# A gated residual tail in another order: two gate products recorded ahead of an out-projection, and a last pair of its own

## The chip, the cores and the metric

The kernel runs on one core of a Trainium2 chip. The metric is the device time of one execution in microseconds (us); a comparison uses the median of several runs. The engines are TensorE (PE; its weight loads are shown apart as PEld), VectorE (DVE), ScalarE (ACT), GpSimd (POOL), and SyncE (SP), whose queue starts every transfer of this kernel.

## The reference, cut to what matters

One decoder layer over 1024 tokens of width 1024, in float32. The last part of it is what the change touches:

```
proj = rms_norm(x) @ w_in                       # split into the columns of both head groups
o_a  = gated delta rule (4 heads, chunks of 64) * silu(a_z)
o_b  = sparse attention (top 256 keys, 8 heads) * silu(b_z)
x = x + concat([o_a, o_b], -1) @ w_out
gate = sigmoid(rms_norm(x) @ w_ple_gate + b_ple_gate)
x = x + (p @ w_ple) * gate
```

## The kernel before, in words

Everything is kept transposed: 128 channels on the partitions, tokens along the free axis, in two halves of 512 tokens (n = 0 and n = 1). A float32 matrix product is made from three products in a fast format: each operand is split into a high part and a low part (`hi`, `lo`; ACT copies the high part, POOL or DVE subtracts to get the low one), and `mm3` issues hi x hi, hi x lo, lo x hi. A product over 512 channels is four `mm3`, so 12 matmuls of 512 columns.

**Out-projection.** `out_job` makes one block of 128 output channels in two parts: the part over the delta-rule heads (jobs oA0 to oA7 for the first half, oC0 to oC7 for the second) and the part over the attention heads (oB0 to oB7, and oD0 to oD7). Jobs oA, oC and oB are fill: they run on PE among the attention's own products. The jobs oD need the attention's last block of 128 queries. That last block ends in `fin`: ACT and DVE bring the sums out of PSUM into `ot`, POOL multiplies by `zt`, ACT makes the high part (`mch` in the trace), POOL the low part (`mcl`).

**Gate.** The gate projection (1024 by 1024) is made for four pairs of output blocks, j = 0 to 3. In each pair, two output blocks and two halves of the tokens form a 2 by 2 block product, done with seven products of 12 matmuls in place of eight (c1 to c7). Two of them, c7 (weights `s3`, tokens `t3`) and c3 (weights `s4`, tokens `b22`), need the first half of the tokens alone: `gate_pre`. The weights `s1` to `s4` are sums and differences of four raw weight blocks r11, r12, r21, r22, made on POOL (`mixed`, tile `mixl`), then split (`sh`, `sl`); `a11`, `a12`, `a22` are raw blocks split as they are (`hiw`, `low`). `f1` and `f2` are intermediate sums that stay in the ring of three `mixl` buffers until `s1` and `s2` are split. `gate_out` finishes a 128 by 512 block: add a part, scale by the row norm, tanh on ACT, two DVE steps, store.

**Order.** Nothing is issued while the Python program runs. It records operations (`Plan.add`), with edges for every data and buffer hazard, and then issues them in a written-out order: `TURNS` is a packed list of 7561 numbers, each the index of the next operation among those still left. Each engine's queue follows that one order. A buffer ring is filled in recorded order, not in issued order. Opening and closing of a buffer pool are operations of that list too:

```
for o in deps:                       # Plan.mark: a pool's closing depends on each use of its tiles
    self.edge(o, op, 2)
...
for k, m in self.marks.items():      # and every opening or closing comes behind the last ones
    self.edge(m, op, 2 if k == key else 0)
...
assert all(p in seen for p in o.pre) # Plan.run: no operation is issued ahead of what it depends on
```

So an operation on a tile of the pool `tail` (`self.tp`: the tiles rawg, sh, sl, p1, u, v) is issued, on its engine, behind every operation of that engine on tiles of the attention's pools, `ot` among them. `raww`, `hiw`, `low` and `mixl` lie in older pools and are not bound by this.

Of the kernel before, what the change touches and what calls it, by code (L numbers as in the profile page):

```python
# [8 lines left out]
F32 = mybir.dt.float32  # L9
# [11 lines left out]
T = 1024  # L21
# [91 lines left out]
Xv*_Jx=wE?kRxU{3>M}1y=xL$+#TGfg_$2g?+FPyxev31O!yRk`hT7l;A#F;Y;g>w(v*cT#^q(VWoM(=<?8k<E-NFO(|s+|nem=0OGf0(|CXuGk+ZF_Oh%V&Nz2rs>4|Wj
$&Tij3M00BI+0AGc_n3UerPRYy~(O7G+2?Q?HWP{i~h>gzocY|snI!9QIUlXAf|!#j3ht657hT5d+5JCq%HDvS8T(!7L^t@Ph0QT7T}hxmKof!E#a8KeOvH?9qYGyxB1Fi
i(6WJt$0gIYogs7YV&RiZ45Q{R!@a0x%KOVp|w-}ZBwCvb)ji;%a&R$-&DPfW14cwqWOJAG)HE6#ymshN%xa&Pgbp5*)(x%as4sRqSPW!M$aSe6Z3{oxS!}fe*Cy9d1A=5
3|;D3z1*{mSUT1|>KoZsJJve7X_Odk85zl$8e2$g9ZigmT=HCm_%q%W8@%U5Pt94;zp?hTJ9a9%R2MJRk()+yLVb8yQ0tCqo!h+yt%M!wngg@2c(*RzjhY6|VrPujdCV!O
KV_)iiZ(;}_y+QEQhS_iuWEy>0B_#ZoZHk4u%(T)jeG24D;y+P#uE1vQ?s**I~&4t27>)N`thuRfdR6#ug_8*0d%1yh$Y6B7&9@qvA^Gpt%)M&daOTGJE+UVYBmySY_O96
crhS5JspI*Z3ep!xLU9_h$3b@f*7zF15)VkhLuQinV|Dcy5YDB-+&SY1e&l-;<->|Q6X(8yTOf6>)=|4ZYXSr6OfZET#$1kF12UP(uh7h6jp~q_LV_7u-vZkSv4N}fIdB4
6N_1qs7Be+NiZa4v}S1H@${T_F<Z22?OK~u7nMrPVab%`(X>IS#VIyno^T!}^AWOEo5H+mgUTFnI-F*`*RI0+o}kXA59C26o~dyg(%q;GW6qdKt+z)+8)eO~)-V=K=Z?4m
1Dy)~nNjvy%#R{^vlRUACgF$rB$P`+v?c(2Wol7fVkXJ=S@pN8NR>`U7MQ-0ZzSKz%QGat%)H6Sca-h6EOM`FxtF<HVFfR~5SDK8eEPNYbpDEzbMaD6&IOtlF3`NBdP+Pc  # L120
M#Qjq9C4g;P)y^a8D2I<L3TgMkU8Z!fCA<U633G`PU9&^NbXA5Dy~L_+D4QIz13RniusM&2JI4(YDUTaMxwWYsGrZ(Q{A;x6BVuQi>jI<6|AJHOR6Z=SLCap7=|jPrMOg>
Bh4W`mt+z;ok&J$o<(TN>B1cjgryl9!yq&bWC{R+kO)DmB?yjCIDzAo64fRWiSlx)thu?Fx(kL8HM(3`6b()>(`a-Avw=u6K^3XZ$th{F=d`qr>{&3fuXo=&@BW|yWdYIw
KwBH#+nYgBv6wcS%*xW_4Y%eYorX9;I9mvsZlsk0EGrQrlU64%O`wr8D3Kina5t_Npq;|hODu&LT7mW%%P>2^TG2vu?)Zd|o6!yxd5n}=S{TysaI;&&d4V9CaJ6NZ3UDcm
QC01(M|3EIR2xK=wOSEMO{i1^s~b}j1S@9Q37eo71rw$1*Ya{NK`y~?R+Edx7ikbl)ajZmHl1kFstgvtMI&>yh}y4ay)jnnwuZGrP=g>e<Kbyp)?$oC^60Snn8u+oL^N2N
%$w|X%%(LWdcCd6rm<T2WP7_st>I9ctutR#bLJY(wA_RkGs@Hk1FNqnQpqf8D@JJ)LHOzvQeB0wn%kgjwC?pr+eap|FO%QBV)mSR#sB)3Z>Po6-1;6Qk(p=6LE<^?EG5(c
&<k7Ba;lngJ&pDVw6!MFoz;y_813t;qnf#<{2my(AIaTL5haLQMZ?0bu5P}*gQrY+CXA^x8;hgqr7CD3tYwfk`-}Z%zoyjdEG_mG(I(pFu+=$4QPgFMMpMA3Evdn33{7=j
yfEm=H&BGH*oPZKEiEnc7qs;Bl;YjNVokkDrNbqJ$71D^G+jf}2uh*`6!qZr;<Ac5T`iiVYD%htQV}Ymb`&u<kt<gn7=}t{4H`sw6fLW%am&i;p|Y2wh##>Wsw}QJNYmEE
1y;O{!>M#DPD)XN$f7a{Je~6iTtre=)Yn&5R@9~{M5oD7VZsZOAtheY`*A}KuEBM9t5Zzkr8z=QPIiGcKMS|;2<CQUhPq-bSfkH#RH>Zh<rtR4XiPK|Vi=F(HvI2%w1k|Q
C*mB5>j=Aw4Pz0#LQtQ~duW{oQc{hLGKpryPLiBOW#P;wM43`@G);<x!%QqAl*Td<f|7&4qk|kop)y`3pVxy?7AIChW-0{D$JRrX)M_X7djHGNZuc5}UczK_BESyW>Tnnh
# [560 lines left out]
class Layer:  # L690
# [1399 lines left out]
    def gate_pair(self, j):  # L2090
# [24 lines left out]
        def second():  # L2115
            parts = []
            for a0, a1 in cuts:
                parts.append(bank(f"c2{j}")[:, :a1 - a0])
                self.product(parts[-1], a12, b21, slice(a0, a1))
# [108 lines left out]
```

## Time and profile before

| what | value |
|---|---|
| median of 3 runs | 819.66 us (819.16 to 820.5) |
| the profiled execution, its own time | 819.92 us |
| its span, first to last instruction | 818.2 us |
| mean granted TensorE clock | 0.995 |
| PE, DVE, ACT, POOL busy | 98%, 76%, 70%, 60% |

The busy shares are means over the whole span. The stretches that the change touches begin at about 640 us, and the attention ends at about 705 us, the products at about 811 us. Lines of the trace all show one source line, so they are told apart by the names of their tiles. A matmul's duration in the timeline holds its latency; the distance from one start to the next is the pace.

### The profile page before, as it was taken

The numbers are of one execution on the slowest core, as the hardware profiler recorded it, in microseconds if no ns is written. First come the engines' busy times: TensorE is split into PE (matmuls) and PEld (weight loads), VectorE is DVE, ScalarE is ACT, GpSimd is POOL, SyncE is SP. The second block draws the span as 40 slices with busy tenths as digits, with TensorE's granted clock in tenths as the row PEclk, the third lists the DMA queues.
The fourth block names the chain that finished last, engine by engine and source line by source line (L and its number), as shares of the span: only waits on it lengthen the run. The fifth ranks groups of instructions, "written<-read, shape, count | busy, mean of one in ns | idle before, by whom it ended". The sixth has DMA issues, their size and how long they took to land.

```text
span 818.2 us, 14758 instructions
## 1 busy us (share of the span) xinstructions
PE 805.2 (98%) x5111; PEld 687.1 (84%) x5111; DVE 618.6 (76%) x1422; ACT 571.4 (70%) x1317; POOL 489.8 (60%) x668
## 2 busy tenths in 40 slices
PE   8999999999999999999999999999999999899996
PEld 6898888888888888888888888888888888688885
DVE  4654446846777889899999988797778788676577
ACT  6653564465568968988999975589767689686342
POOL 3443524232235865766768676758866567899981
PEclk9999999999999999999999999999999999899999
DMA  8953211221111321312322223836543121522453
GB/s 301 372 181 107 89 65 52 86 76 65 45 45 39 92 81 66 86 53 87 103 71 71 85 91 103 268 132 207 180 141 129 65 91 39 167 77 79 140 184 139
DMA packets 77866, 93.14 MB, mean 114 GB/s; under 512 B 24000, under 2 KB 40672, under 8 KB 77664
## 3 DMA queue, kind: packets, MB, share of 16 engines
q1 hardware_dynamic: 77792, 92.20, 34.3%
q8 instruction: 40, 0.66, 0.3%
q14 instruction: 34, 0.28, 0.1%
HBM read 66.72 MB, written 25.45 MB: 113 GB/s over the span
## 4 chain that ended last, share of the span: by engine, by line
PE 92%; ACT 2%; DMA 2%; DVE 2%; issue 1%; SPq 0%; POOL 0%; ACTq 0%
PE mm L557 56%; PE g L557 9%; PE s L557 6%; PE lg L557 6%; PE pv L557 4%; PE S L557 4%; PE pt L557 3%; PE rec L557 3%; PE po L557 2%; DMA xt<-in_x_dram 2%; ACT P L557 1%; DMA pled<-plt 1%; DVE g L557 0%; SPq L557 0%; ACT ot L557 0%
## 5 line engine op out<-in xcount | busy, mean ns | idle before, releaser
L557 POOL TENSOR_TENSOR low<-raww,hiw 128x512 fp32r<-128x512 f32 (+1 forms) x110 | 146.6, 1338 | 138.9 <-ACT hiw L557 133.3
L557 PE MATMUL mm<-hTlo,hiw 128*128 128x512 f32 (+1 forms) x528 | 196.6, 382 | 0.0
L557 PE MATMUL mm<-hThi,hiw 128*128 128x512 f32 (+1 forms) x528 | 195.7, 383 | 0.0
L557 PE MATMUL mm<-hThi,low 128*128 128x512 f32 (+1 forms) x528 | 194.5, 381 | 0.0
L557 PEld LDWEIGHTS mm<-hThi,low 128*128 128x128 f32 x528 | 99.1, 188 | 17.0
L557 PEld LDWEIGHTS mm<-hThi,hiw 128*128 128x128 f32 x528 | 99.1, 188 | 16.1
L557 PEld LDWEIGHTS mm<-hTlo,hiw 128*128 128x128 f32 x528 | 98.9, 188 | 16.2
L557 ACT ACTIVATE junka<-score,nt 128x768 bf16<-128x768 int16 (+5 forms) x96 | 100.0, 1042 | 4.3 <-POOL nt L557 1.5
L557 ACT ACTIVATE hiw<-raww 128x512 fp32r<-128x512 f32 x108 | 67.0, 628 | 30.0 <-PE g L557 11.6
L557 DVE TENSOR_SCALAR_CACHE_REDUCE junk<-score,cand 128x384 bf16<-128x384 f32 (+2 forms) x96 | 71.2, 741 | 1.8
L557 ACT ACTIVATE relu<-lg 128x384 f32<-128x384 f32 (+2 forms) x80 | 39.9, 522 | 44.2 <-PE lg L557 41.6
L557 POOL TENSOR_SCALAR P<-P,rsum 128x128 f32<-128x128 f32 (+7 forms) x64 | 48.8, 771 | 29.4 <-DVE rsum L557 29.2
L557 POOL TENSOR_SCALAR nt<-acca,upa 128x1 f32<-128x1 f32 x96 | 39.5, 414 | 32.6 <-ACT junka L557 28.6
L557 ACT ACTIVATE P<-P,mn 128x128 f32<-128x128 f32 (+7 forms) x64 | 49.4, 772 | 10.5 <-DVE mn L557 9.8
L557 DVE SCALAR_TENSOR_TENSOR score<-relu,sm,score 128x384 f32<-128x384 f32 (+5 forms) x42 | 43.2, 1035 | 16.4 <-ACT relu L557 16.3
L557 DVE TENSOR_TENSOR pl<-pt,ph 128x512 fp32r<-128x512 f32 x72 | 48.0, 684 | 10.0 <-ACT ph L557 7.0
L557 PE MATMUL S<-kst,qT 128*128 128x384 f32 (+2 forms) x192 | 52.6, 348 | 0.0
L557 ACT ACTIVATE ph<-pt 128x512 fp32r<-128x512 f32 x72 | 41.1, 593 | 9.9 <-PE pt L557 8.5
L557 ACT ACTIVATE fst<-mm 128x512 f32<-128x512 f32 (+2 forms) x61 | 30.1, 505 | 22.0 <-PE mm L557 21.9
L557 DVE SCALAR_TENSOR_TENSOR acc<-fst,cw,acc 128x512 f32<-128x512 f32 x48 | 37.4, 791 | 10.0 <-ACT fst L557 5.1
L557 PEld LDWEIGHTS S<-kst,qT 128*128 128x128 f32 x192 | 34.4, 188 | 7.0 <-DVE mn L557 1.4
L557 PE MATMUL pt<-ident,P 128*128 128x128 f32 x288 | 39.9, 273 | 0.4 <-DVE pl L557 0.3
(364 smaller groups left out, 2171.5 us busy)
## 6 DMA issues: line engine op xcount, KB each, us to landing
raww<-in_w_ct_dram SPq DMA_DIRECT2D x66, 256.0 KB
raww<-in_w_out_dram SPq DMA_DIRECT2D x32, 256.0 KB
xt<-in_x_dram SPq DMA_DIRECT2D x8, 512.0 KB
xc<-in_xc_dram SPq DMA_DIRECT2D x8, 512.0 KB
pled<-plt SPq DMA_DIRECT2D x16, 256.0 KB
pld<-pled SPq DMA_DIRECT2D x16, 256.0 KB
out_dram<-gth SPq DMA_DIRECT2D x15, 256.0 KB
rawg<-in_w_gate_dram SPq DMA_DIRECT2D x9, 256.0 KB
```

The costliest lines, as they stand in the source:

```text
L557: r = getattr(getattr(self.nc, o.eng), fn)(*[real(x) for x in args], **{k: real(v) for k, v in kw.items()})
```

## The change

The recorded program changes from the tail on. `gate_pre(0, 0)` and `gate_pre(0, 1)` are now called ahead of all the jobs oD, in place of behind oD2 and oD5. The block r12 of the first pair is loaded into the buffer that `v` uses later, in place of the ring `raww`. The last pair has a function of its own, `gate_last`: its seven products come in the order c1, c2, c7, c6, c4, c5, c3, its weights are made in the order a11, a12, a22, s3, s2, s1, s4, and the product cut into two halves of 256 columns at the very end is c3 in place of c2. In two of its four `gate_out` calls (`late=True`) the last addition is made on POOL. The number of matmuls is the same: seven products in each pair, one of them cut into halves.

`TURNS` is new. Compared as numbers, both lists have 7561 entries; of the first 5,600 entries 114 differ, and from entry 5685 on nearly all do. In the list of before, entry 5685 lies where the attention's fifth of eight blocks of queries begins its transposes, by the count of DVE instructions at about 530 us.

```diff
-        r12 = load(2 * j, 1, self.wp, "raww", 2)
+        r12 = load(2 * j, 1, *((self.wp, "raww", 2) if j else (self.tp, "v", 1)))
...
-        s3 = pair("s", mixed(r11, r21, OP.subtract))
-        f1 = mixed(r21, r22, OP.add)
-        f2 = mixed(f1, r11, OP.subtract)
-        s4 = pair("s", mixed(r12, f2, OP.subtract))
-        yield s3, s4
-        s2 = pair("s", f2)
-        s1 = pair("s", f1)
-        yield s1, s2
-        yield [pair("p", r) for r in (r11, r12, r22)]
+        if j < 3:
...
+        else:
+            yield [pair("p", r) for r in (r11, r12, r22)]
+            s3 = pair("s", mixed(r11, r21, OP.subtract))
+            f1 = mixed(r21, r22, OP.add)
+            f2 = mixed(f1, r11, OP.subtract)
+            s2 = pair("s", f2)
+            f4 = mixed(r12, f2, OP.subtract)
+            s1 = pair("s", f1)
+            yield s3, s2, s1, pair("s", f4)
...
-            nc.vector.scalar_tensor_tensor(p, p, 1.0, pp[:, s], op0=OP.add, op1=OP.mult)
-            nc.vector.tensor_tensor(t[:, s], p, self.x2[n][:, e, s], op=OP.add)
+            q = t[:, s] if late and a1 - a0 == 512 else p
+            nc.vector.scalar_tensor_tensor(q, p, 1.0, pp[:, s], op0=OP.add, op1=OP.mult)
+            (nc.vector if q is p else nc.gpsimd).tensor_tensor(t[:, s], q, self.x2[n][:, e, s], op=OP.add)
...
+    def gate_last(self):
+        nc, j = self.nc, 3
+        (t3, b22), (b11, b21), (t1, t2, t4) = self.h2[0], self.h2[1], self.gt
+        bank = lambda nm: self.tps.tile([128, 512], F32, name=nm, tag="g", bufs=5)
+        keep = lambda nm: self.tp.tile([128, 512], F32, name=nm, bufs=1)
+        gw = self.gate_weights(j)
+        a11, a12, a22 = next(gw)
+        c1, c2 = bank("c13"), bank("c23")
+        self.product(c1, a11, b11)
+        p1 = keep("p1")
+        nc.scalar.activation(p1, c1, AF.Copy)
+        self.product(c2, a12, b21)
+        self.gate_out(2 * j, 1, [c2], p1)
+        s3, s2, s1, s4 = next(gw)
+        c7, c6 = self.mm_ps("c73"), bank("c63")
+        self.product(c7, s3, t3)
+        self.product(c6, s2, t2)
+        u, v = keep("u"), keep("v")
+        nc.vector.tensor_tensor(u, c6, p1, op=OP.add)
+        nc.vector.tensor_tensor(v, c7, u, op=OP.add)
+        c4 = bank("c43")
+        self.product(c4, a22, t4)
+        self.gate_out(2 * j + 1, 1, [c4], v, late=True)
+        c5 = bank("c53")
+        self.product(c5, s1, t1)
+        nc.vector.tensor_tensor(u, u, c5, op=OP.subtract)
+        self.gate_out(2 * j + 1, 0, [c5], v, OP.subtract, late=True)
+        cuts, parts = ((0, 256), (256, 512)), []
+        for a0, a1 in cuts:
+            parts.append(self.mm_ps("c33", a1 - a0))
+            self.product(parts[-1], s4, b22, slice(a0, a1))
+        self.gate_out(2 * j, 0, parts, u, cuts=cuts)
...
-            after = {"oD2": [(self.gate_pre, 0, 0)],
-                     "oD5": [(self.gate_pre, 0, 1)], "oD7": [(self.norm_a, 1), (self.norm_b, 1)]}
+            for k in range(2):
+                self.gate_pre(0, k)
+            after = {"oD7": [(self.norm_a, 1), (self.norm_b, 1)]}
...
-            for j in range(4):
+            for j in range(3):
...
+            self.gate_last()
```

## Rows read from the trace of the kernel before

**Rows 1.** The page: busy time by engine, then two of the lines that cut the span into 40 slices (PE's busy tenths, and the granted TensorE clock in tenths).
```profile
PE 805.2 (98%) x5111; PEld 687.1 (84%) x5111; DVE 618.6 (76%) x1422; ACT 571.4 (70%) x1317; POOL 489.8 (60%) x668
...
PE   8999999999999999999999999999999999899996
...
PEclk9999999999999999999999999999999999899999
```

**Rows 2.** Busy time in five stretches. Columns: the stretch, its length, then busy us and count of instructions of PE, PEld, DVE, ACT and POOL, the granted clock (1.00 is full), the DMA share and GB/s.
```profile
20.00:40.00 20.00, 19.07 (x118) 16.54 (x117) 12.75 (x27) 13.60 (x29) 8.25 (x13) 1.00 1.01 371
...
560.00:704.70 144.70, 144.56 (x775) 121.88 (x774) 118.97 (x295) 112.60 (x223) 101.33 (x91) 1.00 0.34 112
704.70:714.20 9.50, 7.00 (x25) 5.37 (x25) 6.14 (x8) 5.36 (x10) 8.41 (x6) 0.64 0.82 278
714.20:811.50 97.30, 97.27 (x447) 80.99 (x445) 68.43 (x105) 50.49 (x89) 79.81 (x64) 1.00 0.36 120
811.50:818.20 6.70, 0.00 (x0) 0.00 (x0) 3.66 (x9) 0.90 (x2) 0.00 (x0) 0.86 0.39 146
```

**Rows 3.** Timeline of PE around the end of the attention. Columns: start, duration, engine, operation, out<-in, shape, count, and in brackets the idle time before and what ended it.
```profile
701.76 0.39 PE L557 MATMUL mm<-m0Bh,low 128*128 128x512 f32 x1
701.99 0.64 PE L557 MATMUL pt<-ident,P 128*128 128x128 f32 x4
702.38 0.48 PE L557 MATMUL pv<-ph,vst 128*128 128x512 f32 x1
...
704.72 0.50 PE L557 MATMUL pv<-pl,vst 128*128 128x512 f32 x1
706.38 1.24 PE L557 MATMUL mm<-ones,ssum 128*128 128x1 f32 x8 [1.16 <-POOL ssum L557]
708.96 1.22 PE L557 MATMUL g<-mch,hiw 128*128 128x512 f32 x2 [1.34 <-ACT mch L557]
709.98 1.06 PE L557 MATMUL mm<-ident,r 128*128 128x128 f32 x4
...
712.11 0.63 PE L557 MATMUL g<-mch,low 128*128 128x512 f32 x1
712.54 0.63 PE L557 MATMUL g<-mch,hiw 128*128 128x512 f32 x1
...
714.11 0.39 PE L557 MATMUL g<-mch,hiw 128*128 128x512 f32 x1
714.34 0.39 PE L557 MATMUL g<-mcl,hiw 128*128 128x512 f32 x1
```

**Rows 4.** Timeline of ACT, DVE and POOL in the same place: the last block's way from PSUM to the operand of the jobs oD, and the first weights behind it.
```profile
703.17 1.29 POOL L557 TENSOR_TENSOR low<-raww,hiw 128x512 fp32r<-128x512 f32 x1
...
705.25 0.77 ACT L557 ACTIVATE ot<-pv 64x256 f32<-64x256 f32 x2 [0.34 <-PE pv L557]
...
706.06 0.84 DVE L557 TENSOR_TENSOR ot<-ot,pv 64x256 f32<-64x256 f32 x2 [1.39 <-ACT ot L557]
...
706.98 1.26 POOL L557 TENSOR_TENSOR ot<-ot,zt 128x512 f32<-128x512 f32 x1 [0.65 <-DVE ot L557]
...
708.27 0.63 ACT L557 ACTIVATE mch<-ot 128x512 fp32r<-128x512 f32 x1 [1.64 <-POOL ot L557]
...
709.66 1.78 POOL L557 TENSOR_TENSOR mcl<-ot,mch 128x512 fp32r<-128x512 f32 x1
...
716.17 1.30 POOL L557 TENSOR_TENSOR low<-raww,hiw 128x512 fp32r<-128x512 f32 x1 [1.35 <-ACT hiw L557]
```

**Rows 5.** Busy time in three stretches: the last of the attention, and two of the tail (columns as in rows 2).
```profile
680.00:704.70 24.70, 24.70 (x141) 20.52 (x139) 21.25 (x44) 22.66 (x43) 20.43 (x17) 1.00 0.18 54
714.20:760.00 45.80, 45.80 (x210) 38.07 (x209) 30.14 (x45) 32.66 (x59) 42.96 (x35) 1.00 0.27 86
760.00:801.00 41.00, 41.00 (x183) 33.94 (x182) 29.32 (x45) 15.85 (x28) 36.85 (x30) 1.00 0.46 155
```

**Rows 6.** Groups of instructions of POOL from 714.2 to 811.5 us (busy us, mean ns | idle before, releaser), and the last of them in the timeline.
```profile
L557 POOL TENSOR_TENSOR sl<-mixl,sh 128x512 fp32r<-128x512 f32 x16 | 20.6, 1299 | 3.1 <-ACT sh L557 3.1
L557 POOL TENSOR_TENSOR low<-raww,hiw 128x512 fp32r<-128x512 f32 x11 | 14.3, 1299 | 2.4 <-ACT hiw L557 2.4
...
799.60 1.31 POOL L557 TENSOR_TENSOR sl<-mixl,sh 128x512 fp32r<-128x512 f32 x1
```

**Rows 7.** Timeline of the end: the last matmul, DVE instructions from 811.36 us on, one tanh on ACT, and the stores.
```profile
811.19 0.28 PE L557 MATMUL g<-h1Bh,low 128*128 128x256 f32 x1
...
811.36 0.69 DVE L557 SCALAR_TENSOR_TENSOR g<-g,pld 128x512 f32<-128x512 f32 x1
...
812.30 0.68 DVE L557 TENSOR_TENSOR gth<-g,x 128x512 f32<-128x512 f32 x1
812.89 0.42 DVE L557 TENSOR_TENSOR g<-p,g 128x256 f32<-128x256 f32 x1
...
814.01 0.45 ACT L557 ACTIVATE g<-g,bg 128x256 f32<-128x256 f32 x1 [1.14 <-DVE g L557]
814.50 0.43 DVE L557 SCALAR_TENSOR_TENSOR g<-g,pld 128x256 f32<-128x256 f32 x1 [0.20 <-ACT g L557]
814.96 0.42 DVE L557 TENSOR_TENSOR gth<-g,x 128x256 f32<-128x256 f32 x1
...
811.15 4.60 SPq L557 DMA_DIRECT2D out_dram<-gth  x4
```

More of the change, by code (lines that the diff above doesn't have):

```diff
@@ new lines @@
+WHKA&5_}m(lgS92CX>!3&bMH`4Q9Jszd_LJwI+?;Xw+wCXInJ7cwEv&qZ**eH0XjsjY$JCGSmi(pckAb!6pi@+F;U)^H8f@S~;^$2A^e$$KzT)8r4SNuqHE8PzT|FnimA8
+!1J8dYUc!tQ4*BAp4TEun+6sHmXGr$o;R>6ol2!vDL9pjb30vDr^4Y-*kPMwu|yQGlqpFeCSYPR5Rqo}T2|}U!Wy-jf*1p%Cyg||Os^mqo?#eP{wX7hpDP%Kq-omnQ<`>5
+H0O{w&d70`mZJ?opeTl+Xa!9xm4reL%YO(PMR_TbBw3a<u&ka?DvfGVq0n-2!E#|7I}Zh;n1`fNi3$ayRLWt7QQfOm!Kmf~GUTkZ{DEW$g+fQlr3>V;Wi&x$Q51#AZK5-2
+x|^m^it3PK2tp79f*>S<z;OePY2-v0L9j%l97*`(e2eCrh00Xv=^Axr`2NqGuX}rIJ@$+j?7_?+$W+7HZ@>1@*yPv3Z+!o!p`ZOj-`4BR#h>WH?MDg1LlhBtxD!vJm<`Lu
@@ new lines @@
+P&6)~Xao(j=sl3A8kK8DS(Qpq@jS0msa#quYv<KgtJ<PAn^{S!udkQ6GbW9Wj+(2hC3b~>*yUm)^XzdJrJX8AjzeWvB@;H4Rb{b+Rc4hGRGIuLpBTJH5U0uEa*0lt#c6d|
+?elE2S_j?B@4*^bX$yz7W@|7QwCKWeuuYqjBQ?p$&K4WoS@Y;32D<wDHL++f))VO-F2tDmtc6AQP<anaD?2)(6>a$fO7q;duC5fjOtI-FKjD77Rz`b4Tie9M<m8!&)2BCI
+xIjOB5&qjHqf3^YTXOdN#J84=d&VZmn3E^Jdzv}re)0?>zs{V=+$KM$(>D$DldsdXidG-zKK!tc>Fs5D&h^kMR-9h3YSpTvM^_y|mK{F)`pQF(KKkgD70#nakt4KPeO<2O
+I7^?qb!*?vORpcnGEmeY<IW?`zxw?1uShRneesPK@0#zvAie&&^yZu9L$~knuSze!^2&h&FTM5}dFMs`?p<>4>#ALEzWEn-cHKS5yz<H$uiSn2-48yv`yXz8_2y0XyZc|=
@@ new lines @@
+$}6kOE6d8668Iy!xM==}J)eR|5`&VdWHKAdPUWUji9}8ULr^$|#IGl^kXSexhGVgKESwq1%!DJSLg7d_l!-<n5hNT8gaR1in+K913m4)>AQueVT`rh|EikNrMR?A553B0y
+Pj2^k91fSuz459C7(_#(snH}!qG+?%*3~y$#-77OFKmRj>K6>qeSLip)sqF{AT|-hqCl<=q|;n}enUe;CSZd>P#vhMYGo_40`Yht7F$phE3B!B1=vnFABLBN;Kjw%EqQnB
+DlE)#)uq$Hd{3oMp`ezuMoJixvBnFSV~jb<FmRX#6%_<jR%Qn!IELx4?di1S&&%8FlroZ~8Iso<SI10lx7no$iXaY&5Kuvo*j)q(kYIu!h}J?0B8wnmF-<gD!$NdsCTbw{
+v<^F|1sduxHJg7lAH{N&vQwc*vWSwJzx!YiOrWB?-_OdX%P1vTuR`fYTvn&kNjV%AjI>%U0Bi%0D8WWiM2$wn0}mMFa`k%HifFYCRAaMY!zDw;!NEb}@{)lfw6D+5D~KXu
+)X9pW)5lx&Ivt8*AvBC;Dng-<0u2Q6OBlaD<!5}pgc7B349z0YSSYFwh4ExEQ^IAhG#K?oOyMw!g+g90@Stw57u9#@68C`IyK=|^^^UlvR->shYh*ze{IVIKdzXS#j;w~D
@@ L148 @@
+2mMj({3R|pUtj_V`ooO_{d#Di&yyzz`kk@+GzR)i-hZlz&~KLZdG-A={pS$rH&XvHH}r+%gFe%d&llTYmk0eGi$R~yN$B(S`&SzV=(n~FUqEo^^DF+0MWD})74$oW|0)jp
+&4K&PvHWbR-)c1UJH3Uza324jB@FuQ4nd#k2n79Zvfsyn`?!D9^6v)7FRY0J2$wmIpeX)t!Sc`_d90!PbiR-K;&~tczYYDDbu4?IWcTs!6#oykG{1=
 """
@@ L2051, in mixed @@
             return f
-        s3 = pair("s", mixed(r11, r21, OP.subtract))
-        f1 = mixed(r21, r22, OP.add)
-        f2 = mixed(f1, r11, OP.subtract)
-        s4 = pair("s", mixed(r12, f2, OP.subtract))
-        yield s3, s4
-        s2 = pair("s", f2)
-        s1 = pair("s", f1)
-        yield s1, s2
-        yield [pair("p", r) for r in (r11, r12, r22)]
+        if j < 3:
+            s3 = pair("s", mixed(r11, r21, OP.subtract))
+            f1 = mixed(r21, r22, OP.add)
+            f2 = mixed(f1, r11, OP.subtract)
+            s4 = pair("s", mixed(r12, f2, OP.subtract))
+            yield s3, s4
+            s2 = pair("s", f2)
+            s1 = pair("s", f1)
+            yield s1, s2
+            yield [pair("p", r) for r in (r11, r12, r22)]
+        else:
+            yield [pair("p", r) for r in (r11, r12, r22)]
+            s3 = pair("s", mixed(r11, r21, OP.subtract))
+            f1 = mixed(r21, r22, OP.add)
+            f2 = mixed(f1, r11, OP.subtract)
+            s2 = pair("s", f2)
+            f4 = mixed(r12, f2, OP.subtract)
+            s1 = pair("s", f1)
+            yield s3, s2, s1, pair("s", f4)
     def product(self, ps, w, b, s=slice(0, 512)):
@@ L2065, in product, with gate_out @@
             self.mm3(ps, hi[:, k], lo[:, k], bh[:, k, s], bl[:, k, s], k == 0, k == 3)
-    def gate_out(self, e, n, ps, part=None, op=OP.add, cuts=((0, 512),)):
+    def gate_out(self, e, n, ps, part=None, op=OP.add, cuts=((0, 512),), late=False):
         nc, a = self.nc, self.a
@@ L2112, in gate_pair @@
         self.gate_out(2 * j, 0, [c3], u)
-        cuts = ((0, 512),) if j < 3 else ((0, 256), (256, 512))
[L2115 to L2119, printed above, removed]
-            self.gate_out(2 * j, 1, parts, p1, cuts=cuts)
-        if j < 3:
-            second()
+        c2 = bank(f"c2{j}")
+        self.product(c2, a12, b21)
+        self.gate_out(2 * j, 1, [c2], p1)
         c4 = bank(f"c4{j}")
@@ L2125, in gate_pair @@
         self.gate_out(2 * j + 1, 1, [c4], v)
-        if j == 3:
-            second()
+    def gate_last(self):
[9 more added lines that the diff above has]
+        nc.scalar.activation(p1, c1, AF.Copy)
+        self.product(c2, a12, b21)
+        self.gate_out(2 * j, 1, [c2], p1)
+        s3, s2, s1, s4 = next(gw)
[17 more added lines that the diff above has]
+        self.gate_out(2 * j, 0, parts, u, cuts=cuts)
     def tail(self):
```

125 lines of the change are left out of this document (55 added, 70 removed).

## The prediction

> **What bounds the kernel now.** I read the page first. PE is busy for 98% of the span and the others for 76% or less [rows 1]: PE sets the time, and what can be won is what PE loses, to idleness or to a slow clock. The line of slices shows where that is: PE's tenths drop in the first slice, in the thirty-fifth and in the last two, and the granted clock drops in the thirty-fifth alone [rows 1]. The table by stretches sharpens this [rows 2]. From 560 to 704.7 us PE idles 0.14 us in 144.7, from 714.2 to 811.5 us 0.03 us in 97.3, both at a clock of 1.00. Between them lies a stretch of 9.5 us with 7.0 us busy and a clock of 0.64, and behind them one of 6.7 us with no matmul at all. I call the first the seam and the second the end.
>
> The timeline of PE shows the seam from inside [rows 3]. The attention's last product starts at 704.72 us. Then PE waits for POOL's sum of squares (1.16 us), runs eight one-column matmuls, waits for ACT's `mch` (1.34 us), and starts the first product of job oD0 at 708.96 us. That wait has a chain behind it [rows 4]: ACT takes the last sums out of PSUM at 705.25, DVE to 706.90, POOL multiplies to 708.24, ACT splits to 708.90. So from the last product to the first oD product is about 4.0 us (704.95 to 708.96), and the chain is bare latency, no engine's load. Behind it matmuls of 512 columns start 0.43 us apart (712.11 to 712.54) and from 714.11 on 0.23 us apart [rows 3]; these are the two clock levels, 1.2 and 2.4 GHz, and PE stood idle twice before the low one.
>
> What the seam costs: in its 9.5 us lie about twelve matmuls of 512 columns (2.7 us at 0.23), four transposes (0.39 us, by 701.99 to 702.38) and the eight one-column matmuls (1.24 us as measured at the seam; I take 0.4 at full pace, an estimate between nothing and that) [rows 3]. That is 3.5 us of work, so 6.0 us are lost: 2.5 in the two waits, 3.5 in pace.
>
> **The change, part by part.** *Matmuls.* None is added or removed: each pair keeps seven products, one product is still cut in two. Cost 0; what can change is only when PE is idle.
>
> *c7 and c3 ahead of the oD jobs.* Read plainly, this puts 24 matmuls (24 x 0.23 = 5.5 us) that need only the first half into the seam. The profile with the code says they can't go there. Their weights lie in `sh`, `sl` and the raw blocks in the pool `tail`, which opens behind every use of the attention's tiles; the last use is POOL's `mcl` of `ot`, at 709.66 [rows 4]. Behind it POOL must subtract (1.29), ACT split (0.63), POOL subtract again (1.30) [rows 4, 6]. Even with `mcl` directly behind `mch` (708.90 + 1.3 = 710.2) c7's high products start at 710.2 + 1.3 + 0.6 = 712.1 us and its low ones at 713.4, while oD0 can start at 708.96. So this move fills nothing before 709; by itself it is worth 0 at the seam. All that it issues moves with it: 24 matmuls, 2 splits on ACT, 6 POOL instructions (two each for s3 and s4, and `f1`, `f2`), 4 loads on SP's queue. These now lie among the first oD weights, and they bring a tighter ring: the price is the second rival. The r12 load in `v`'s buffer costs nothing: `v` is first written after c6, long after the split of r12.
>
> *New order from about 530 us on.* This can fill the seam. Fill and attention share 144.7 us in which PE is never idle [rows 2], and fill products run until 701.76, 3 us ahead of the attention's end [rows 3]. If one product of the first half (twelve matmuls) is held back behind the last attention product, the attention ends about 2.7 us earlier and the same PE work covers 2.7 of the 4.0 us. Room for it exists, if narrow: from 680 us on DVE is busy for 21.25, ACT for 22.66, POOL for 20.43 of 24.7 us [rows 5], and a fill job that is held back takes its own ACT and DVE work along. Bounds: 0 (fill as before) and the whole 6.0. With 10 to 12 matmuls held back and 0.4 us for the one-column ones, 2.8 of 4.0 us are covered and 1.2 remain. Whether the clock holds decides the other half. The nearest row is 20 to 40 us: 0.93 us of idleness and a clock of 1.00 [rows 2]. I take that the clock holds: 6.0 - 1.2 = 4.8 us won. The Trainium skill ("TensorE: Matmul & The Clock Gate", "Part 1: The HAM clock gate") says that the array falls to half clock after an idle stretch and is given the full clock after sustained work; the seam's 0.64 agrees. By it a seam that is closed in part may keep the whole slow stretch; the first rival is that case.
>
> *Last pair.* Its `s` weights were POOL's last work, ending at 800.9 us [rows 6] while PE had 10.6 us to go; now the last weights, s4, serve the last product alone, of 24 half-width matmuls. POOL is 94% busy from 714.2 to 760 and 90% to 801 [rows 5], so a PE that comes 5 us earlier needs POOL to keep up; the new order gives it some 7 us more room. Worth 0 by itself, since PE waits for nothing there now, but without it the seam's gain could be given back here.
>
> *End.* The last matmul starts at 811.19 and DVE touches the last half only at 812.89, behind 0.69 and 0.68 us of an earlier block [rows 7]. `late` takes two additions (0.68 each) from DVE and gives POOL two (1.3 each), where POOL has nothing left to do. But c5 adds its own subtraction (0.69) near the end. Bounds 0 and 1.4 us; I take 0.7. The last chain itself (five steps, store to 818.2) stays.
>
> Sum against the profiled execution: 819.92 - 4.8 - 0.7 = 814.4 us. The median is 0.26 us lower, so 814.2 to 814.4; I say 814.3.
>
> **Rivals.** *The clock falls all the same.* The idle time at the seam shrinks but the slow stretch stays: 2.5 - 1.2 = 1.3, with the end 2.0 us: 817.7. For it speaks that only 2.5 us of waits brought 3.5 us of slow pace; against it the 0.93 us above.
>
> *The `mixl` ring holds the oD jobs back (slower).* `f1` and `f2` are now recorded ahead of all oD jobs and keep two of three `mixl` buffers until s1 and s2 are split; oD1's square comes next in that ring. oD jobs have five PSUM banks, and oD0 needs no `mixl`. So PE can run oD0 to oD5, c7 and c3, 96 matmuls or 22.1 us from 708.96, to 731.0; then oD6 needs oD1's bank, so its square and copies, some 2 us of ACT and DVE work. By 729 POOL must have made, from 708.9 on: `mcl`, the last low part of t3, the row norm's power, six for s3 and s4, two for s2 and s1, five `low`: 16 instructions at 1.30 us [rows 6], 20.8 us, to 729.7. It decides from where POOL's waits and extras there exceed nothing at all; it is late by one instruction at once. In the order before, three squares lie ahead of `f1`, so five banks serve the five jobs behind them. Price: one instruction late, 1.3 us of idleness, and at the seam's rate (3.5 us of pace for 2.5 us of waits) 1.8 more, less the end's 0.7, if the seam stays: 819.7 + 2.4 = 822.1. Against it: PE had no waits in 97 us of the tail [rows 2] though POOL was 94% busy in its first half [rows 5], and an oD weight can be made later in favour of s1.
>
> *The seam stays.* Fill is spent before the attention ends, as now; c7 and c3 come where other work was ready anyhow. Only the end moves: 819.0. For it: the recorded move can't reach the seam, and DVE and ACT have 3.5 and 2.0 us left in the attention's last 24.7 [rows 5]. Against it: from 560 to 704.7 us they have 26 and 32 us left [rows 2].
>
> **How the numbers follow.** Forecast (seam mostly closed) 0.41, 812.9 (whole 6.0 and 0.7 more at the end) to 816.5; the clock falls 0.14; seam stays 0.25; the ring or another new wait 0.20. About 0.2% (1.6 us) is what a measurement of this kernel can tell from no change: faster is below 818.0, slower above 821.3. Faster: the forecast and most of the first rival, 0.41 + 0.10 = 0.51. Same: the seam that stays, the rest of the first rival, 0.25 + 0.04 = 0.29. Slower 0.20. The range leaves out the far part of the slower case and a tenth below: 812.9 to 822.4.
>
> **What would show it.** In the changed kernel: `mm` products of the first half behind the last `pv` product; less than 1.5 us of PE idleness between that and oD0's first product; a granted clock of 1.00 there; `sh` products starting 3 us or more behind oD0's first product, not ahead of it; PE without waits until the end; the last DVE step closer to the last matmul than now (3.8 us). Wrong would make it: a new wait of PE some 20 us behind the seam (for a bank, or for POOL's `low` or `sl`), or fill that still ends ahead of the attention.

## The result, and the profile after

The changed kernel took 815.53 us (median of 6 runs, 814.8 to 817.23) against 820.22 us before (6 runs, 819.16 to 821.17): a ratio of 0.9946, 95% interval 0.9933 to 0.9959. That is 4.4 us less by the ratio and 4.7 between the two medians. Forecast was 814.3 us, range 812.9 to 822.4, faster at 0.51. The profiled execution has a span of 814.4 us against 818.2.

The page of the changed kernel, in the same lines as [rows 1], and its waits of PE from 600 us to the end (columns: who waited for whom, us in total, times, longest):

```profile
PE 802.3 (99%) x5111; PEld 685.0 (84%) x5111; DVE 615.7 (76%) x1420; ACT 572.6 (70%) x1317; POOL 493.2 (61%) x670
...
PE   8999999999999999999999999999999999999996
...
PEclk9999999999999999999999999999999999999999
```

```profile
PE g L557 <- ACT mch L557: 1.2, 1, 1.2
```

The dent in the thirty-fifth slice is gone, in PE's busy tenths and in the clock. Two additions have gone from DVE (1422 to 1420) to POOL (668 to 670), and one wait of PE is left of the two. The table by stretches, with columns as in [rows 2]; the second row is the seam, the fourth the end:

```profile
560.00:702.60 142.60, 142.58 (x770) 121.15 (x769) 118.50 (x297) 111.82 (x220) 100.99 (x90) 1.00 0.35 113
702.60:709.20 6.60, 5.34 (x22) 3.65 (x21) 3.64 (x5) 5.42 (x10) 4.70 (x5) 1.00 0.78 254
709.20:808.30 99.10, 99.05 (x460) 82.37 (x458) 70.23 (x110) 52.50 (x93) 85.84 (x68) 1.00 0.40 134
808.30:814.40 6.10, 0.00 (x0) 0.00 (x0) 2.88 (x7) 0.90 (x2) 1.26 (x1) 0.71 0.28 101
```

Where 0.64 of the full clock was granted, it is now 1.00, and PE idles 1.26 us there. The timeline of PE in the changed kernel shows what fills the seam:

```profile
702.29 0.46 PE L557 MATMUL pv<-pl,vst 128*128 128x512 f32 x1
702.58 0.40 PE L557 MATMUL mm<-m0Bl,hiw 128*128 128x512 f32 x1
...
704.87 0.39 PE L557 MATMUL mm<-m0Bh,low 128*128 128x512 f32 x1
...
706.50 1.47 PE L557 MATMUL g<-mch,hiw 128*128 128x512 f32 x4 [1.25 <-ACT mch L557]
...
708.44 0.39 PE L557 MATMUL g<-mch,hiw 128*128 128x512 f32 x1
...
715.93 0.95 PE L557 MATMUL mm<-ones,ssum 128*128 128x1 f32 x8
716.74 0.71 PE L557 MATMUL g<-mch,hiw 128*128 128x512 f32 x2
...
719.32 0.39 PE L557 MATMUL mm<-mch,sh 128*128 128x512 f32 x1
```

The last attention product starts at 702.29 us. Behind it come eleven `mm` products of job oB7, of the first half, to 704.87; then one wait of 1.25 us for `mch`; then oD0. The eight one-column matmuls of the row norm, which stood in the seam in [rows 3], come at 715.93, between other products. The first gate product with a weight `sh` starts at 719.32, 12.8 us behind oD0. The chain from the last attention product to `mch` is as bare as in [rows 4]:

```profile
702.78 0.77 ACT L557 ACTIVATE ot<-pv 64x256 f32<-64x256 f32 x2 [0.80 <-PE pv L557]
...
704.51 1.28 POOL L557 TENSOR_TENSOR ot<-ot,zt 128x512 f32<-128x512 f32 x1 [1.16 <-DVE ot L557]
704.97 1.37 DVE L557 SCALAR_TENSOR_TENSOR m0Bl<-x,g,m0Bh 128x512 fp32r<-128x512 f32 x1 [0.54 <-ACT m0Bh L557]
...
705.82 0.63 ACT L557 ACTIVATE mch<-ot 128x512 fp32r<-128x512 f32 x1 [0.89 <-POOL ot L557]
...
706.53 1.28 POOL L557 TENSOR_TENSOR mcl<-ot,mch 128x512 fp32r<-128x512 f32 x1 [0.74 <-ACT mch L557]
```

The end, against [rows 7]:

```profile
807.97 0.28 PE L557 MATMUL mm<-m0Bh,sl 128*128 128x256 f32 x1
...
808.98 1.26 POOL L557 TENSOR_TENSOR gth<-gth,x 128x512 f32<-128x512 f32 x1 [2.06 <-DVE gth L557]
809.14 0.42 DVE L557 TENSOR_TENSOR mm<-u,mm 128x256 f32<-128x256 f32 x1
...
811.02 0.42 DVE L557 TENSOR_TENSOR gth<-mm,x 128x256 f32<-128x256 f32 x1
```

DVE comes to the last half 1.17 us behind the last matmul's start (1.70 before), and its last step starts 3.05 us behind it (3.77 before).

**A table by stages.** One profile's start can differ from another's by some tenths: here the changed kernel's first `pv` product starts at 531.41 us, that of before at 530.73, though what lies ahead is nearly the same. (On PE the two orders are the same up to 594.9 us of before; what is new for PE begins there, later than the 530 us of the list, and well ahead of the 640 us named above.) So I cut all runs at four instructions of PE and compare the distances between their starts: from the first `pv` to the last `pv` (the attention from its first such product on), to oD0's first product (the seam's chain), to the last matmul (the tail), and to the end of the span (the end). The differences of starts are worked out from each run's timeline; the runs below the second row are the experiments. There is one profile of each kernel. Kernels that share an order differ by up to 0.6 us in a stage (the attention takes 173.93 to 174.50 us in one order, 170.88 to 171.24 in the other), so a difference of a few tenths in one stage shows nothing by itself.

| kernel | attention | chain | tail | end | sum | ratio to before |
|---|---|---|---|---|---|---|
| before | 173.99 | 4.24 | 102.23 | 7.01 | 287.47 | 1 |
| after | 170.88 | 4.21 | 101.47 | 6.43 | 282.99 | 0.9946 |
| old_last_pair | 171.24 | 4.20 | 101.66 | 7.09 | 284.19 | 0.9954 |
| last_pair_alone | 174.32 | 4.24 | 102.83 | 6.16 | 287.55 | 0.9994 |
| fill_alone | 170.91 | 4.20 | 115.66 | 7.23 | 298.00 | 1.0135 |
| fill_alone_2 | 170.94 | 4.25 | 105.44 | 8.76 | 289.39 | 1.0030 |
| old_fill | 174.07 | 4.27 | 109.91 | 6.56 | 294.81 | 1.0099 |
| old_fill_2 | 174.50 | 4.28 | 105.83 | 6.25 | 290.86 | 1.0051 |
| hold_one_job | 173.42 | 4.30 | 108.40 | 7.04 | 293.16 | 1.0081 |
| keep_busy | 173.93 | 4.25 | 101.11 | 7.05 | 286.34 | 0.9984 |
| last_mult_on_dve | 171.07 | 3.58 | 101.82 | 6.44 | 282.91 | 0.9936 |
| no_late | 171.07 | 4.22 | 101.69 | 7.25 | 284.23 | 0.9963 |

After against before: 3.11 us in the attention, 0.03 in the chain, 0.76 in the tail, 0.58 at the end: 4.48 us, near the 4.4 to 4.7 that the runs say. The gain shows in the attention because work left it; the chain's 4.2 us stay and are filled. The groups of PE between the first and the last `pv` say which work. First the kernel before, then the changed one (count, then busy us and mean ns):

```profile
L557 PE MATMUL mm<-m0Bh,low 128*128 128x512 f32 x32 | 12.9, 402 | 0.0
L557 PE MATMUL mm<-m0Bl,hiw 128*128 128x512 f32 x32 | 12.6, 400 | 0.0
L557 PE MATMUL mm<-m0Bh,hiw 128*128 128x512 f32 x32 | 12.2, 397 | 0.0
```

```profile
L557 PE MATMUL mm<-m0Bh,hiw 128*128 128x512 f32 x29 | 11.4, 406 | 0.0
L557 PE MATMUL mm<-m0Bl,hiw 128*128 128x512 f32 x28 | 11.2, 400 | 0.0
L557 PE MATMUL mm<-m0Bh,low 128*128 128x512 f32 x28 | 11.2, 398 | 0.0
```

96 products became 85; all other groups have the same counts in both. Eleven at 0.23 us are 2.5 of the 3.1 us; the other 0.6 us is the same work packed closer.

### The profile page after: what moved, and what is told of

Its sections match the earlier page's. It is cut to its first block, busy times and chain, and to the rows that moved or that the text cites. A ratio compares the mean times of both kernels' runs of the same rounds, so it can differ in the third digit from the quotient of the medians.

```text
span 814.4 us, 14745 instructions
## 1 busy us (share of the span) xinstructions
PE 802.3 (99%) x5111; PEld 685.0 (84%) x5111; DVE 615.7 (76%) x1420; ACT 572.6 (70%) x1317; POOL 493.2 (61%) x670
## 4 chain that ended last, share of the span: by engine, by line
PE 90%; DMA 3%; ACT 3%; DVE 2%; POOL 1%; issue 1%; SPq 0%; ACTq 0%
PE mm L557 53%; PE g L557 9%; PE s L557 6%; PE lg L557 6%; PE pv L557 4%; PE S L557 4%; PE pt L557 4%; PE rec L557 3%; PE po L557 2%; DMA xt<-in_x_dram 2%; DMA pled<-plt 1%; ACT P L557 1%; DMA Qt<-qd 1%; POOL rs L557 0%; SPq L557 0%
```

## The experiments

Each is compared with the kernel before. A kernel whose recorded program or order differs needs an order of its own. In those that mix the two orders (`fill_alone`, `old_fill` and their second versions) and in `hold_one_job` I wrote the order behind the attention anew, and in the other runs on the last pair that of the end. It is less good than the two that came with the kernels: the totals hold waits of my making, so the stages have to decide. `last_mult_on_dve` alone has the changed kernel's `TURNS` as it is.

**1. The fill's order alone, and its reverse.** `fill_alone` is the program of before; attention and fill are issued in the order of after. `old_fill` is the program of after with the attention and the fill in the order of before.

```diff
-TURNS = order of before
+TURNS = order of after up to the attention's last operation, then the tail's operations of before
```

> The recorded program of before (c7 and c3 behind oD2 and oD5, old last pair), issued up to the attention's last product exactly as the changed kernel does; behind that the order of before, fitted to it. Theory (the gain at the seam comes from the first half's fill that now lies behind the attention's last product): oD0 starts some 2.5 us earlier than before and the granted clock holds; -2.5 to -4 us, 816.2 to 817.7. Rival (c7 and c3 recorded ahead are needed for the gain): no gain, 819 to 821, with new waits behind the seam.

> The recorded program of the changed kernel, issued up to the attention's end as before does (no fill behind the last product), then its own order. Theory (fill): the seam is as in before, 2.5 us of waits and a slow clock; only the end moves, 819.2 to 820.2. Rival (c7 and c3 ahead, or the new last pair, carry the gain): 816 to 817.5.

Measured: 831.51 us, ratio 1.0135 (1.0117 to 1.0153), and 828.57 us, ratio 1.0099 (1.0082 to 1.0117). Both are slower than before and outside what was expected (816.2 to 817.7 and 819.2 to 820.2), so neither total shows a gain of the fill. By stages they part: with the fill of after the attention takes 170.91 us, with that of before 174.07, whatever the program. The losses lie in the tail. PE's waits in `fill_alone`:

```profile
PE g L552 <- DVE t1l L552: 5.4, 1, 5.4
PE g L552 <- ACT x L552: 2.8, 1, 2.8
PE g L552 <- ACT mch L552: 1.3, 1, 1.3
PE g L552 <- POOL mcl L552: 1.1, 1, 1.1
```

The longest goes back to SP's queue (start and length of an entry, its waiting included):

```profile
693.00 14.00 SPq L552 DMA_DIRECT2D raww<-in_w_out_dram  x3
...
708.99 6.26 SPq L552 DMA_DIRECT2D x<-x1d  x8
```

and through it to DVE, which waits for the loads of `x` (timeline of DVE in `fill_alone`):

```profile
716.04 0.70 DVE L552 TENSOR_TENSOR g<-x,g 128x512 f32<-128x512 f32 x1 [3.42 <-DMA x<-x1d]
```

Three weight loads stand in the queue until their buffers come free, and the loads of `x` behind them leave at 708.99 us; in the changed kernel the first four leave at 704.15. That was a fault of my order, so the pair was made again.

**2. The same pair, with loads of `x` ahead of the weight loads that wait.** SP's loads in `fill_alone`, and in `fill_alone_2`, in order of issue:

```diff
-raww, raww, raww, raww, rawg, rawg, rawg, x, x, x, x, x, x, x, x
+raww, raww, raww, rawg, rawg, x, x, rawg, raww, x, raww, x, x, raww, x, x, x
```

> As fill_alone (program of before, attention and fill issued as in the changed kernel), but with the loads behind the seam ordered anew, so that no load of x1d stands behind a weight load that waits for its buffer. Theory (the held-back fill is the gain): oD0 2.5 to 3 us earlier than before and no long wait behind it; 816.5 to 818.5. Rival (c7 and c3 recorded ahead are needed to carry PE over the first 25 us behind the seam): new waits of PE of 2 us and more in all, 819 and more.

> As old_fill (program of the changed kernel, attention and fill issued as before), with the loads behind the seam ordered anew in the same way. Theory: the seam costs what it cost before, only the end is shorter; 819 to 820.5. Rival (the recorded move brings a gain by itself): below 818.

Measured: 822.72 us, ratio 1.0030 (1.0020 to 1.0040), and 824.42 us, ratio 1.0051 (1.0037 to 1.0066). The tail of `fill_alone_2` is 10 us shorter than that of `fill_alone` (105.44 against 115.66), so the queue was the fault; 4 us more than in the changed kernel remain, and the end is longer too. Both theories missed on the total, and `fill_alone_2` shows its rival's sign: over 819 us, with 2.1 us of new waits of PE behind the seam (0.9 for DVE's `t1l`, 0.9 for POOL's `mcl`, 0.3 for POOL's `low`). Attention: 170.94 and 174.50 us. What follows: the 3.1 us of the attention go with the fill's order, in four kernels out of four. What is not shown is that the fill is enough for the whole gain. Of these four kernels and the changed one, the last alone is faster than before, and it alone has the new fill, the new program and an order made for both; whether the program of before would win with the new fill and a better order of the tail, or needs c7 and c3 recorded ahead to carry PE behind the seam, stays open, and no run here has it.

**3. The last pair.** `old_last_pair` is the changed kernel with the last pair made by the loop as before; `last_pair_alone` is the kernel before with the new last pair alone.

```diff
-            for j in range(3):
+            for j in range(4):
...
-            self.gate_last()
```

> The changed kernel with the last pair as before (c2 last, weights s first, no addition on POOL). Theory: the end alone goes back, +0.5 to +1.0 us on the changed kernel, 816.0 to 816.6, and PE still has no wait between the seam and the end. Rival (the new last pair gives POOL the room without which the seam's gain is given back): PE waits for POOL near 790 us, over 817.5.

> The kernel before with the new last pair alone. Theory: from the last matmul to the end 0.6 us less, 819.4 to 819.8, PE's waits as before. Rival (its order costs PE waits, since s4 comes last): 821 and more.

Measured: 816.7 us, ratio 0.9954 (0.9940 to 0.9968), and 819.75 us, ratio 0.9994 (0.9982 to 1.0006). Without the new last pair the end is 0.66 us longer (7.09 against 6.43), and PE's only wait is still that for `mch`, 1.3 us: POOL kept up with the old order of the weights too. The last pair alone shortens the end by 0.85 us, loses 0.60 in the tail under my order, and is no measurable change. So its worth is the end, about 0.7 us, and it isn't needed to keep the seam's gain. The totals are too near each other to say it (the intervals of `old_last_pair` and the changed kernel overlap); the stage says it, for the end takes 6.16 to 6.56 us in each kernel whose last pair has `late` and 7.01 or more in each without.

**4. One job held back, locally.** `hold_one_job` is the program of before; the twelve matmuls of one first-half job are issued behind the last attention product, and its neighbours keep their places.

```diff
-mm x6, pv, mm, pv x2, pt x8, mm x8, pt x8, pv x5, mm, pt x4, pv, pt x4, mm, pv x2, mm, pt x4, pv, pt x4, pv x7
+mm x5, pv, mm, pv x2, pt x16,              pv x5,     pt x4, pv, pt x4,     pv x2,     pt x4, pv, pt x4, pv x7, mm x12
```

These are PE's instructions from about 693 us to the last `pv`, by the tiles they write (`mm` of the fill alone).

> The kernel before with one edit of the order: the twelve matmuls of oB7 stand behind the attention's last product, what depends on them follows, and the attention itself is issued as before. The prediction's step: the attention then ends 2.7 us earlier and the seam closes; 815.5 to 817.5. Rival (the attention's last block is bound by its own chain over ACT and DVE, so PE only idles ahead of its last product instead): its last product within 0.5 us of where it is before, no gain, 819.5 to 823.

Measured: 827.2 us, ratio 1.0081 (1.0066 to 1.0096). The seam is filled: the clock is 1.00 in the ten us behind the last `pv`, and one wait of 1.06 us is left. But the attention takes 173.42 us, 0.57 less than before, not 2.7, and kernels of one order differ by as much. That is the rival's mechanism; the total lies above both ranges. The timeline of PE in `hold_one_job` shows why:

```profile
697.62 1.26 PE L552 MATMUL pt<-ident,P 128*128 128x128 f32 x8 [1.33 <-DVE pl L552]
...
702.02 0.66 PE L552 MATMUL pt<-ident,P 128*128 128x128 f32 x4 [0.37 <-DVE pl L552]
```

Where the fill is taken out, PE runs into the attention's own chain (transpose, split on ACT, low part on DVE, product). The fill products had covered that latency. In the changed kernel PE waits nowhere in the attention from 600 us on, with eleven products fewer: its order was made anew from about 595 us on. The tail of this run has five waits more, of my order.

**5. The clock by itself.** `keep_busy` is the kernel before with fourteen added matmuls of 384 columns, seven in each of the seam's two waits. Nothing reads what they write.

```diff
+                if i == 7:
+                    junk = pp.tile([128, 512], F32, name="junk", tag="S", bufs=2)
+                    for _ in range(14):
+                        nc.tensor.matmul(junk[:, :384], hi[:, 1, 0:128], hi[:, 0, 0:384], start=True, stop=True)
```

> The kernel before with 14 matmuls of 384 columns added that nothing reads, seven in each of PE's two waits at the seam (2.4 us of work where PE waits 2.5). The critical chain is the same, oD0 can start no earlier. Theory (the slow pace behind the seam is the clock, which falls since PE stood idle): the granted clock at the seam stays near 1.00 and some 2 to 3.5 us come back, 816.7 to 818.2. Rival (the pace there is set by operands that come late): no gain, 819.5 to 821.

Measured: 818.97 us, ratio 0.9984 (0.9975 to 0.9992), 1.3 us less: between what the theory and the rival said. The stretch from 704 to 714 us (columns as in [rows 2]), first of before, then of `keep_busy`:

```profile
704.00:714.00 10.00, 7.50 (x27) 5.52 (x26) 6.81 (x9) 6.06 (x11) 8.68 (x7) 0.66 0.78 263
```

```profile
704.00:714.00 10.00, 9.12 (x46) 6.59 (x45) 7.28 (x10) 6.33 (x12) 8.71 (x7) 1.00 0.73 253
```

The clock stays full, the chain is as long as before, and the tail is 1.12 us shorter. What the full clock runs into is seen in PE's timeline behind the seam of `keep_busy`, and then in PE's, DVE's and POOL's of the kernel before:

```profile
709.24 0.74 PE L552 MATMUL g<-mch,hiw 128*128 128x512 f32 x2 [0.18 <-ACT mch L552]
...
711.78 0.50 PE L552 MATMUL g<-mcl,hiw 128*128 128x512 f32 x1 [0.66 <-POOL mcl L552]
...
713.27 0.40 PE L552 MATMUL g<-mch,hiw 128*128 128x512 f32 x1
```

```profile
711.68 0.63 PE L557 MATMUL g<-mcl,hiw 128*128 128x512 f32 x1
```

```profile
708.20 1.48 POOL L557 TENSOR_TENSOR r<-r,mhalf 128x4 f32<-128x4 f32 x1
...
709.55 0.75 DVE L557 SCALAR_TENSOR_TENSOR m0Bl<-x,g,m0Bh 128x512 fp32r<-128x512 f32 x1
```

The first product that needs `mcl` starts at 711.68 us in before, at the low clock and without a wait of PE, and at 711.78 in `keep_busy`, at the full clock and behind a wait of 0.66. Counted from oD0's first product (708.96 and 709.24) that is 2.72 us against 2.54. So in before two limits end almost together: the slow pace of the matmuls ahead, and `mcl`, which POOL has ready at 711.44 [rows 4]. The full clock takes the first away, and the second stays: POOL's power of the row norm (1.48 us) stands between the multiplication and `mcl`, which then takes 1.78 us. Up to there the clock costs 0.18 us. The next six steps take 2.43 us in before, to 714.11 [rows 3], and 1.49 in `keep_busy`, to 713.27: 0.94 us. Together that is the 1.12 us of the tail. In the changed kernel `mcl` follows `mch` directly (706.53, 1.28 us), and the row norm comes later.

**6. What is left of the seam, and `late`.** `last_mult_on_dve` moves one instruction of the changed kernel; `no_late` gives both additions back to DVE.

```diff
-                nc.gpsimd.tensor_tensor(ot, ot, zt, op=OP.mult)
+                (nc.vector if i == 7 else nc.gpsimd).tensor_tensor(ot, ot, zt, op=OP.mult)
```

```diff
-        self.gate_out(2 * j + 1, 1, [c4], v, late=True)
+        self.gate_out(2 * j + 1, 1, [c4], v)
...
-        self.gate_out(2 * j + 1, 0, [c5], v, OP.subtract, late=True)
+        self.gate_out(2 * j + 1, 0, [c5], v, OP.subtract)
```

> The changed kernel with one instruction moved: the last block's multiplication of `ot` by `zt` is made on DVE in place of POOL. In the changed kernel POOL takes 1.28 us for it, from 704.51 to 705.79, and PE then waits 1.25 us for ACT's `mch` before oD0 starts at 706.50; behind the wait the first products are 0.3 us and more apart while POOL's `mcl` (706.53 to 707.81) is outstanding. DVE takes 0.68 us for a multiplication or addition of 128x512 from SBUF, and is idle from 704.43 to 704.97. Theory (what is left of the seam is the bare latency of the last block's chain): oD0's first product comes about 0.6 us earlier behind the last attention product, PE's wait falls from 1.25 to about 0.6 us, `mcl` moves as far, and the whole kernel is about 0.6 us faster than the changed one: 0.993 to 0.994 of the time before. Rival (behind the seam something else holds PE: the weights `hiw`, DVE's `m0Bl`, or a slow clock): the wait shrinks, but PE loses as much within the next 10 us, and the time stays that of the changed kernel, 0.9946 of before.

> The changed kernel without `late`: in the last pair both additions that POOL made are made on DVE again; the order is otherwise kept as near as it goes. In the changed kernel the last matmul starts at 807.97 us and the last DVE step at 811.02, 3.05 us later; before it was 3.8. Theory (`late` is what shortens the end, since DVE had 0.69 and 0.68 us of an earlier block in front of the last half): the last DVE step comes about 3.7 us behind the last matmul, and the kernel is 0.6 to 0.9 us slower than the changed one: 0.9955 to 0.9965 of before. Rival (the end is shorter because the order of the last products changed, or because the last product is c3 in place of c2): no change, about 3.05 us and 0.9946 of before.

Measured: 814.76 us, ratio 0.9936 (0.9924 to 0.9949), and 817.05 us, ratio 0.9963 (0.9951 to 0.9975). In `last_mult_on_dve`:

```profile
704.24 0.69 DVE L552 TENSOR_TENSOR ot<-ot,zt 128x512 f32<-128x512 f32 x1
704.85 0.74 DVE L552 SCALAR_TENSOR_TENSOR m0Bl<-x,g,m0Bh 128x512 fp32r<-128x512 f32 x1
...
705.64 1.48 PE L552 MATMUL g<-mch,hiw 128*128 128x512 f32 x4 [0.61 <-ACT mch L552]
...
721.15 0.19 PEld L552 LDWEIGHTS g<-mch,hiw 128*128 128x128 f32 x1 [0.44 <-DVE t1l L552]
```

The wait falls from 1.25 to 0.61 us and the chain from 4.21 to 3.58, as the theory has it: what is left of the seam is bare latency. The tail gives 0.35 us back, some of it in a new gap between the weight loads at 721.15 behind DVE's `t1l`. The median is the lowest of all kernels here, but its interval and that of the changed kernel overlap: better by 0.1% is likely, not shown.

`no_late` ends so:

```profile
807.75 0.28 PE L553 MATMUL mm<-m0Bh,sl 128*128 128x256 f32 x1
...
810.26 0.68 DVE L553 TENSOR_TENSOR gth<-g,x 128x512 f32<-128x512 f32 x1
...
811.19 0.74 DVE L553 TENSOR_TENSOR gth<-mm,x 128x256 f32<-128x256 f32 x2
```

The last DVE work ends 4.18 us behind the last matmul's start, where it was 3.47 with `late` and 4.19 before, with the same product last. So the end's gain is `late`: DVE's 0.68 us additions in front of the last half. Nothing is seen there of the new order of the products, though the order of DVE's other steps at the end isn't quite the same in the two kernels. The 0.82 us of that stage are what is shown; the intervals of the totals overlap.

## Why the prediction was right, and where its sizes were off

**The place and the mechanism held.** PE was the bound, the gain is the seam and the end, and all that was to show it is there: first-half products behind the last `pv`; 1.25 us of idleness there (1.2 forecast); a clock of 1.00; `sh` products far behind oD0; no later wait of PE; the last DVE step closer. The words of the change, c7 and c3 ahead of the oD jobs, fill nothing before oD0, as the prediction read from the pool `tail`: POOL's subtraction for s3 comes at 710.72 us and the first `sh` product at 719.32.

**The seam: 4.8 forecast, 3.9 measured** (3.11 + 0.03 + 0.76). Two terms were mis-sized. The eight one-column matmuls were taken at 0.4 us of work; at full clock the next matmul starts 0.81 us behind them (715.93 to 716.74), so before only 5.6 us were lost, not 6.0. And the prediction kept 1.2 us of loss afterwards; the wait of 1.25 us is that, but oD0's first six products take 1.94 us (706.50 to 708.44), where six at 0.23 are 1.38. The clock there is 1.00. What they wait for is seen in the weight loads (PEld) of the changed kernel:

```profile
707.02 0.53 PEld L557 LDWEIGHTS g<-mch,hiw 128*128 128x128 f32 x3 [0.33 <-ACT hiw L557]
707.86 0.19 PEld L557 LDWEIGHTS g<-mcl,hiw 128*128 128x128 f32 x1 [0.32 <-POOL mcl L557]
```

The second product waits for ACT's `hiw`, which ACT makes behind `mch`, and the fifth for POOL's `mcl`. So most of these 0.56 us are waiting for operands, which the prediction had put at nothing. Together 0.97 us, about the 0.9 that are missing.

**The pace: 3.5 us were not the clock's.** The step "these are the two clock levels" took every wide gap for the clock. By `keep_busy` the clock's share is 1.1 to 1.3 us, and 0.4 are the one-column matmuls. Another 1.2 lie between oD0's first product and the first on `mcl`: four products and four transposes are 1.3 us at full pace, and took 2.54 in `keep_busy`, where the clock was full, because `mcl` came late. Most of the other 0.8 us was no pace at all. The busy time of a stretch holds the latency of the last matmul ahead of each wait: the one-column ones are listed with 1.24 us and take 0.81, the last `pv` with 0.50 and takes 0.23 [rows 3], 0.7 us in all. Had the clock fallen in a seam that is otherwise closed, the cost would have been some 1.2 us, by the estimate from `keep_busy`, not the 3.5 of the first rival. The forecast came out near in part by luck: the new order removes the late `mcl` too, and that part of the gain was counted under a wrong name. (One line is misread besides, without weight for the sum: PE's tenths drop in the last slice alone, not in the last two [rows 1].)

**"If one product is held back, the attention ends 2.7 us earlier" is not true by itself.** `hold_one_job` did just that, and its attention is shorter by 0.57 us. The prediction saw room in the busy shares of DVE and ACT [rows 5]; what counts is the latency between them that the fill covered. The new order keeps it covered: there eleven products fewer did make the attention 3.11 us shorter.

**The `mixl` ring did not hold.** From `mcl` at 706.53 POOL has split s1 by 726.0 us, 19.5 us later, against 20.8 estimated, and PE waits for none of it. The rival's kind is real all the same: with the same fill and a worse order behind it, `fill_alone_2` lost 4.0 us in the tail and `fill_alone` 14.2, against the changed kernel.

**The end: 0.7 forecast, 0.58 measured, and the last pair 0 by itself otherwise.** `old_last_pair` and `no_late` agree: 0.66 and 0.82 us in the end's stage, and no wait of PE behind the seam without the new order of weights. "Without it the seam's gain could be given back" did not come true.

## What to carry to other kernels

Where PE waits on a chain of bare latency, look for work that can be moved into the wait, and size the gain by that work's own matmuls: the chain keeps its length, and the stage that the work leaves becomes shorter, if what is left there still covers its own latencies. A seam is judged by three things told apart (idle time, clock, operands that come late), since a wide gap between matmuls can be either of the last two. And a moved job moves its loads: in SP's queue one load that waits for its buffer held back each load behind it (14.00 us in `fill_alone`).

## What the runs showed of the hardware

**DVE and POOL block each other.** In the changed kernel DVE's `m0Bl` (two tiles from SBUF) takes 1.37 us beside POOL's multiplication, and 0.74 us in `last_mult_on_dve`, where POOL is idle. The next one, and POOL's instructions around it, in the changed kernel:

```profile
707.77 1.29 POOL L557 TENSOR_TENSOR low<-raww,hiw 128x512 fp32r<-128x512 f32 x1
...
708.36 1.25 DVE L557 SCALAR_TENSOR_TENSOR m0Bl<-x,g,m0Bh 128x512 fp32r<-128x512 f32 x1 [1.42 <-ACT m0Bh L557]
...
709.02 1.75 POOL L557 TENSOR_TENSOR ssum<-ssum,mixl 128x512 f32<-128x512 f32 x1
```

DVE ends 0.55 us behind POOL's `low` (709.61 and 709.06), and POOL's next one takes 1.75 us in place of 1.30. The Trainium skill ("SBUF — State Buffer", "Who interferes with whom") has DVE and GpSimd share one pair of ports as an exclusive lock that the loser waits for; the trace agrees, in both directions. The late `mcl` of the kernel before is a case of it: DVE's `m0Bl` starts 0.11 us ahead of it (709.55 and 709.66) and takes its 0.75 us, while `mcl` takes 1.78 us in place of the 1.28 it takes in the changed kernel. So an instruction moved from POOL to DVE can free a neighbour as well.

**The clock forgave more than expected.** In the ten us behind the last `pv` the granted clock is 0.66 in before, whose waits are 1.16 and 1.34 us with one-column matmuls between, but 1.00 in `fill_alone`, with waits of 1.3 and 1.1 us around products of 512 columns, and 1.00 in the changed kernel with 1.25. As much idle time costs the clock in one place and not in the other; what stands between the waits differs. Kernels with the old seam got 0.66 to 0.83 in these ten us (`old_fill` 0.67, `old_fill_2` and `last_pair_alone` 0.83), each from one profile. The Trainium skill ("TensorE: Matmul & The Clock Gate", "Part 1: The HAM clock gate") sets the clock by how busy the array has been recently; that fits, and no run here says more.
